# Token-major gates and branches, a finer hand-written order, and block transposes on VectorE in a two-layer hybrid decoder

## The chip, the cores and the metric

One core of one Trainium2 chip runs the whole program. The metric is device time in microseconds of one execution, as the median of the runs of a kernel. The core has five engines that work side by side, each on its own queue of instructions in order: TensorE (matmuls and transposes through the matmul array, into PSUM), VectorE, ScalarE (activation functions and copies), GpSimd (here only powers and a few fills), and SyncE (SP), which issues nearly all DMAs. The rows call them PE, DVE, ACT, POOL and SP; PEld is TensorE's weight load.

## The reference

The input is x, 256 tokens of 1024 features in float32. Each of two layers computes, with its own weights:

```
proj = x @ w_in                       # 1024 -> 7704 columns
ya = rg_lru(conv(proj[a])) * gelu(proj[a_gate])           # 512 wide
yb = rms_norm(gated_delta_rule(q, k, v)) * silu(proj[z])  # 512 wide
yc = rms_norm(gla(q, k, v)) * silu(proj[r])               # 512 wide
gates = sigmoid(proj[merge] + gate_b)                     # 3 x 1024
merged = sum(gates[b] * (y_b @ w_branch[b]) for b in (a, b, c))
x = layer_norm(alpha * x + merged @ w_out)
x = layer_norm(alpha * x + (silu(x @ w1) * (x @ w3)) @ w2)   # 2816 hidden
```

The gated delta rule solves, for each head and chunk of 64 tokens, a unit lower triangular system; the kernel builds the inverse from blocks of 8 up to 128.

## The kernel before

Every operand of a large product is split into a high and a low part of TensorE's fast float32 form, and each product is three matmuls: high x high, high x low, low x high. Weights come as 292 units of 128 x 1024 floats (512 KB), in the order of `ORDER`. `load_w` (line 402) issues a unit's DMA on SP into one of four `raw` buffers; `split_w` (line 415) makes the high part `hi` on ScalarE and the low part `lo` on VectorE, and then issues the next load; `unit` (line 441) hands out the next ready unit, after `fill` has brought the count of ready units up to `ahead` (6, and 14 from the first step of the last branch).

Two forms of product use a unit. Feature-major (`fm_acc`, `fm_pair`, line 1183) holds a 128x128 block of weights in the array and streams 256 tokens of x: 24 matmuls of 256 columns a unit, with features on the partitions of the result. Token-major (`tm_acc`, line 469, `tm_group`, line 1149) holds 128 tokens of x and streams 512 columns of weights: 12 matmuls of 512 columns a unit, with tokens on the partitions. The first FFN products of hidden columns from 512 up (`fm_acc2`, line 461, tile `f`) hold weights and stream the high and low part of x as one operand of 512 columns, and then the high part alone (256) against the low weights; in the tile of x (`xtile`, line 479) the high and low part of one block of 128 features lie 512 floats apart.

The order of work is written out by hand. `MIX` (line 42) lists the steps of a layer's mixer: `c`, `k`, `q`, `v`, `ax`, `ag`, `z` are projections, `gA0` to `gA3` the gates of branch A (each step 256 columns, two units), `bA0` the branch product of 256 columns (one unit), and so on for C and B. `main` (line 1191) walks the list and yields between units; everything else is a chain (a generator), such as `b_inv` (line 644, the inverse and what follows), `a_chain`, `c_chain`, `ln_chain` (line 1030). `Order` (from line 155) holds a model of each engine's clock. Its `drive` (line 211) traces, at each yield of `main`, the next step of a chain whose due time by the model has come. So the position of every instruction on its engine's queue is fixed when the program is traced. The SP queue is kept in the program's order.

Gates: `g_chain` (line 1003) applies a sigmoid with a per-feature bias on ScalarE, two activations of 128x256 a step. Branches: `m_chain` (line 1015) multiplies the product by the gate and adds it to `macc` on VectorE; after the last branch it splits the sum into `mh` and `ml`, which are the held operand of `wo`. `wo` runs the column halves one after the other; its last six units are done for the first 128 tokens and then for the second, so that the norm of the first runs beside the second.

Inverse: in `b_inv` `Y` is the transposed inverse so far, and `X` is its transpose. `X` is made three times a layer from blocks of at most 32, by 8 transposes on TensorE (tile `px`) and two copies on ScalarE.

## Time and profile before

| | us |
|---|---|
| median of 3 runs | 939.6 |
| lowest, highest | 938.99, 940.14 |
| the profiled execution | 940.46 |
| its span, first to last instruction | 938.7 |
| TensorE busy | 924.4 |
| VectorE busy | 642.0 |
| ScalarE busy | 527.6 |
| weight loads: 512 KB each, us to landing (median) | 4.4 |

The span runs from the first to the last instruction of the profiled execution; the rest of its time lies around it. Layer 0 runs to about 466 us. In it the projections run to about 120 us, the inverse stage beside the first gates to 174, branches and gates to 257, `wo` to 280, the FFN from there. The same stages of layer 1 begin at 466, end at 633, 721 and 744. Matmuls are pipelined, so the busy time of one is longer than the distance from one to the next; the chain in order of time shows that distance.

### The profile page before, as it was taken

Reading aid. Unit: us, or ns where it says so; the run is one execution under the profiler, and the core shown is the slowest. Engines: PE = TensorE matmul, PEld = TensorE weight load, DVE = VectorE, ACT = ScalarE, POOL = GpSimd, SP = SyncE. Lnnn points to the kernel's source line nnn. Section 1 sums busy time; section 2 is a strip of 40 time slices with the busy share of each in tenths; the row PEclk is TensorE's granted clock in tenths of the full one; section 3 lists DMA queues with packets and bytes.
Section 4 is the critical chain, followed back from the end, with each engine's and each line's share of the span. In section 5 each row is a group of like instructions: output and inputs, shape, how many; then the busy total and the mean of one; then the engine's idle time right before and its main releaser. Section 6 shows DMA issues by size and latency. Waiting matters only on the chain.

```text
span 938.7 us, 15760 instructions
## 1 busy us (share of the span) xinstructions
PE 924.4 (98%) x6306; PEld 840.3 (90%) x6306; DVE 642.0 (68%) x1017; ACT 527.6 (56%) x827; POOL 29.0 (3%) x29
## 2 busy tenths in 40 slices
PE   8999999999999999999999999999999999999996
PEld 5999999999988888888889999989999888888885
DVE  6778976675865776675557879574768658666715
ACT  5867679535724755565045864973457147555600
POOL 1000100000000000000000020000100000000001
PEclk9999999999999999999999999989999999999999
DMA  8855243545851865578144444234468248555801
GB/s 284 257 183 154 78 149 94 186 166 193 297 222 67 281 213 186 193 244 264 54 156 140 144 146 131 95 122 149 158 240 285 105 138 280 187 179 180 291 1 45
DMA packets 47993, 162.84 MB, mean 173 GB/s; under 512 B 7536, under 2 KB 8496, under 8 KB 47792
## 3 DMA queue, kind: packets, MB, share of 16 engines
q1 hardware_dynamic: 47776, 161.71, 51.5%
q8 instruction: 49, 0.80, 0.3%
q14 instruction: 24, 0.20, 0.1%
q10 hardware_dynamic: 144, 0.13, 0.0%
HBM read 160.77 MB, written 1.05 MB: 172 GB/s over the span
## 4 chain that ended last, share of the span: by engine, by line
PE 91%; ACT 4%; DVE 2%; DMA 1%; issue 1%; POOL 0%; SPq 0%; POOLq 0%; DVEq 0%; ACTq 0%
PE fm L346 25%; PE f L346 22%; PE w L346 13%; PE tm L346 11%; PE br L346 7%; PE wo L346 5%; DMA raw<-in_w_dram 1%; ACT L291 1%; PE pt L346 1%; PE pp L346 1%; DVE lo L303 1%; PE pln L354 1%; PE co L346 1%; ACT hi L291 1%; PE ptm L354 0%
## 5 line engine op out<-in xcount | busy, mean ns | idle before, releaser
L303 DVE TENSOR_TENSOR lo<-raw,hi 128x1024 fp32r<-128x1024 f32 (+1 forms) x293 | 350.8, 1217 | 94.4 <-ACT hi L291 88.1
L291 ACT ACTIVATE hi<-raw 128x1024 fp32r<-128x1024 f32 (+1 forms) x293 | 300.6, 1053 | 79.5 <-DMA raw<-in_w_dram 64.6
L346 PE MATMUL fm<-x,hi 128*128 128x256 f32 x1536 | 282.9, 286 | 0.0
L346 PEld LDWEIGHTS fm<-x,hi 128*128 128x128 f32 x1536 | 240.1, 192 | 2.3 <-issue 1.6
L346 PE MATMUL fm<-x,lo 128*128 128x256 f32 x768 | 217.6, 283 | 0.0
L346 PE MATMUL f<-x,hi 128*128 128x512 f32 x576 | 203.8, 399 | 0.0
L346 PE MATMUL f<-x,lo 128*128 128x256 f32 x576 | 161.8, 281 | 0.0
L346 PEld LDWEIGHTS fm<-x,lo 128*128 128x128 f32 x768 | 147.7, 192 | 0.0
L346 PEld LDWEIGHTS f<-x,hi 128*128 128x128 f32 x576 | 108.2, 188 | 26.9
L346 PE MATMUL w<-hi,hh 128*128 128x512 f32 (+1 forms) x396 | 111.1, 367 | 0.0
L346 PEld LDWEIGHTS f<-x,lo 128*128 128x128 f32 x576 | 108.8, 189 | 0.1
L346 PE MATMUL tm<-hi,x 128*128 128x512 f32 x320 | 100.7, 398 | 2.1 <-ACT hi L291 2.1
L346 PEld LDWEIGHTS w<-hi,hh 128*128 128x128 f32 x396 | 71.4, 189 | 12.3
L346 PEld LDWEIGHTS tm<-hi,x 128*128 128x128 f32 x320 | 59.3, 190 | 15.3 <-ACT hi L291 3.8
L346 PE MATMUL w<-lo,hh 128*128 128x512 f32 (+1 forms) x198 | 72.4, 366 | 0.0
L346 PE MATMUL tm<-lo,x 128*128 128x512 f32 x160 | 62.2, 392 | 0.1
L291 ACT ACTIVATE gt<-fm,vecs 128x256 f32<-128x256 f32 x48 | 20.5, 470 | 48.0 <-PE fm L346 48.0
L346 PEld LDWEIGHTS w<-lo,hh 128*128 128x128 f32 x198 | 37.3, 188 | 6.2
L291 ACT ACTIVATE x<-pln 128x256 fp32r<-128x256 f32 x24 | 7.9, 383 | 61.7 <-PE pln L354 61.7
L346 PE MATMUL wo<-hi,mh 128*128 128x512 f32 x128 | 39.8, 392 | 0.0
L303 DVE TENSOR_TENSOR hv<-f,hv 128x256 f32<-128x256 f32 x36 | 15.2, 422 | 31.4 <-ACT hv L291 31.4
L346 PEld LDWEIGHTS tm<-lo,x 128*128 128x128 f32 x160 | 30.2, 189 | 7.1 <-DVE lo L303 0.7
(276 smaller groups left out, 1081.8 us busy)
## 6 DMA issues: line engine op xcount, KB each, us to landing
raw<-in_w_dram SPq DMA_DIRECT2D x291, 512.0 KB, 4.4
lnv<-in_lnv_dram SPq DMA_DIRECT2D x8, 512.0 KB, 8.0
xr<-in_xtm_dram SPq DMA_DIRECT2D x1, 1024.0 KB, 7.4
xin<-in_xfm_dram SPq DMA_DIRECT2D x3, 256.0 KB, 7.0
raw<-in_w_dram SPq DMA_DIRECT2D x2, 256.0 KB, 3.4
ar<-in_aw_dram SPq DMA_DIRECT2D x8, 64.0 KB, 3.9
out_dram<-xr SPq DMA_DIRECT2D x2, 256.0 KB, 2.1
kc<-in_kc_dram SPq DMA_DIRECT2D x1, 476.0 KB, 8.9
```

What stands on the lines that cost most here:

```text
L291: ins_ = A.activation(o, i, f, **k)
L303: V.tensor_tensor(out=o, in0=a, in1=b, op=op)
L346: T.matmul(o, w, x, start=start, stop=stop)
L354: T.transpose(o, i, idn)
```

## The change

The gates become token-major: a step is now 512 columns (four units), the bias is added on VectorE from a tile `gbias` that is broadcast over the partitions by a DMA of 512 KB (one for each branch and layer), and a sigmoid of 128x512 follows on ScalarE. The branch products become token-major too, two units a step. The merged sum is therefore token-major; it is transposed on TensorE (tile `pmt`) and split from PSUM into `mh` and `ml`. `wo` runs by rows of its weights first and columns second, and waits for the merged halves `mrg00`, `mrg01`, `mrg10`, `mrg11`. The prefetch depth grows by 1 at the two C steps, by 2 at the two B steps, and to 14 at `wo`.

The order's model now keeps, for each piece of a tile, who wrote and read it and when, and takes due times from that; its costs are new; token-major groups, feature-major units and `w2` yield after half a unit. In the tiles of x the high and low part of a block of 128 features lie side by side. The three transposes of the inverse become one `transpose` of 128x1024 in blocks of 32x32 on VectorE (`flip`).

Not shown below: the packing of weights and bias in the new order, the cost terms of the remaining helpers (each now names its operands), and the same in the loads at the start.

```diff
-MIX = ("c0 c1 ax0 k0 k1 q0 z0 q1 ax1 v0 v1 ag0 ag1 gA0 gA1 gA2 gA3 bA0 bA1 bA2 bA3 "
-       "gC0 bC0 gC1 bC1 gC2 bC2 gC3 bC3 gB0 gB1 bB0 bB1 gB2 bB2 gB3 bB3").split()
+MIX = ("c0 c1 ax0 k0 k1 q0 z0 q1 ax1 v0 v1 ag0 ag1 gA0 gA1 bA0 bA1 gC0 bC0 gC1 bC1 "
+       "gB0 gB1 bB0 bB1").split()
...
-            o += fm(C_MG + 1024 * b, i) if nm[0] == "g" else [("br", b, i)]
-    o += [("wo", n, q) for n in range(2) for q in range(4)]
+            o += tm(C_MG + 1024 * b + 512 * i) if nm[0] == "g" else [
+                ("br", b, i, q) for q in range(2)]
+    o += [("wo", n, q) for q in range(4) for n in range(2)]
...
-    def op(self, eng, cost, ready=0.0):
-        t = max([self.clk[eng], self.ready, ready] +
-                [f for e, f in self.fin.items() if e != eng])
-        t += cost
-        self.clk[eng] = t
-        self.fin[eng] = t
+        self.ready = self.last = ready
+
...
+    def op(self, eng, occ, tail=0.0, out=None, ins=(), ready=0.0):
+
+        t = max(self.clk[eng], self.ready, ready)
+        for a in ins:
+            t = max(t, self.after(eng, a, False))
+        if out is not None:
+            t = max(t, self.after(eng, out, True))
+        self.clk[eng] = t + occ
+        f = t + occ + tail
...
+        return f
+
     def end(self):
-        return max(list(self.fin.values()) + [self.ready])
+        return self.last
...
-    def dve(o, x=0.0):
-        O.op("dve", 0.13 + x + 0.00104 * n_of(o))
+    def dve(o, *i, x=0.0):
+        n = max(n_of(a) for a in (o,) + i)
+        ps = any(a.space == bass.MemoryType.PSUM for a in i)
+        O.op("dve", 0.045 + x + 0.057 * ps + 0.00104 * n, 0.105, o, i)
...
+    def flip(o, i):
+
+        V.transpose(o, i)
+        dve(o, i)
...
         if w.dtype == F32R:
-            O.op("pe", max(n, m, 128) / 2400.0)
+            c = max(n, 2 * m) / 2400.0 + 0.0135
         else:
-            O.op("pe", max(n, m, 32) / 600.0)
+            c = max(n, m, 24) / 600.0 + 0.01
+        O.op("pe", c, 0.16, o, (w, x))
 
     def tp(o, i, idn):
         T.transpose(o, i, idn)
-        O.op("pe", 0.107)
+        O.op("pe", 0.109, 0.16, o, (i,))
...
-    def load_w(between=None):
+    def dma(o, i, free=0.0):
+        nc.sync.dma_start(out=o, in_=i)
+        O.clk["dma"] = max(O.clk["dma"], free + 1.5)
+        keep, O.ready, last = O.ready, 0.0, O.last
+        f = O.op("dma", o.shape[0] * n_of(o) * 4 / 285e3, 0.5, o)
+        O.ready, O.last = keep, last
+        return f
...
+        t = raws.pop(0)
...
     def xtile(name):
-        v = [slot(name, F32R).rearrange("p (q k c) -> p k q c", q=2, k=2) for _ in range(4)]
+        v = [slot(name, F32R).rearrange("p (k q c) -> p k q c", q=2, k=2) for _ in range(4)]
         return [t[:, :, 0] for t in v], [t[:, :, 1] for t in v], v
...
             tt(YT.rearrange("p (t b i) -> p t b i", t=8, b=16),
                z[:, :, None, :].to_broadcast([P, 8, 16, 8]), b16, MULT)
             yield
-            for tk in range(2):
-                px = h4(bank("px"))
-                for h in range(4):
-                    tp(px[:, h], Y[tk][:, h], ident)
-                cp(X[tk], px)
+            flip(XT, YT)
...
                 yield
-                for tk in range(2):
-                    px = h4(bank("px"))
-                    for h in range(4):
-                        tp(px[:, h], Y[tk][:, h], ident)
-                    cp(X[tk], px)
+                flip(XT, YT)
...
-        def g_chain(ps, b, j):
-            ps = p2(ps)
-            if j % 2 == 0:
-                B["gt", b, 0], B["gt", b, 1] = pair2("gt")
-            gt = B["gt", b, j % 2]
-            for t in range(2):
-                act_fn(gt[:, t], ps[:, t], AF.Sigmoid, bias=vc(V_GB + 8 * b + 2 * j + t))
-            B["gg", b, j] = gt
-            done(f"gt{b}{j}")
-            return
-            yield
-
-        def m_chain(ps, n, b, j, mh, ml):
-            yield k_(f"gt{b}{j}")
-            ps = p2(ps)
-            gt = B["gg", b, j]
+        def g_tm(ps, b, j, tk, bias):
+            if tk == 0:
+                B["gt", b, j] = pair("gt")
+            gt = B["gt", b, j][tk]
+            tt(gt, ps, bias[:, 512 * j:512 * j + 512], ADD)
+            yield
+            act_fn(gt, gt, AF.Sigmoid)
+            done(f"gt{b}{j}{tk}")
+
+        def m_tm(ps, n, b, j, tk, mh, ml):
+
+
+            yield k_(f"gt{b}{j}{tk}")
+            gt = B["gt", b, j][tk]
             if n == 0:
-                if j % 2 == 0:
-                    B["macc", j], B["macc", j + 1] = pair2("macc")
-                tt(B["macc", j], ps, gt, MULT)
-            else:
-                tt(gt, ps, gt, MULT)
-                tt(B["macc", j], B["macc", j], gt, ADD)
-            if n == 2:
-                split(mh[j], ml[j], B["macc", j])
-                done(f"mrg{j}")
+                if j == 0:
+                    B["macc", tk] = pair("macc")
+                tt(B["macc", tk][j], ps, gt, MULT)
+                return
+            tt(gt, ps, gt, MULT)
+            acc = B["macc", tk][j]
+            tt(acc, acc, gt, ADD)
+            if n == 1:
+                return
+            yield
+            pt = h4(bank("pmt"))
+            for q in range(4):
+                tp(pt[:, q], acc[:, q * P:(q + 1) * P], ident)
+            for q in range(2):
+                split(*(x[2 * j + q][:, :, tk * P:(tk + 1) * P] for x in (mh, ml)),
+                      pt[:, 2 * q:2 * q + 2])
+            done(f"mrg{j}{tk}")
...
                         w = unit(2)
                         for tk in range(2):
                             tm_acc(ps[tk], x, tk, w, 2 * q, q == 0, q == 3)
-                        if q == 3:
-                            for tk in range(2):
+                            if q == 3:
                                 O.spawn(chain(ps[tk], tk), 1)
-                        yield
+                            yield
...
                             fill()
-                        if q % 2:
-                            yield
+                        yield
...
-                fm_acc(p2(ps)[:, t], unit(8), xs)
-                if t:
-                    O.spawn(chain(ps), prio)
-                yield
+                w = unit(8)
+                for k in range(0, 8, 4):
+                    fm_acc(p2(ps)[:, t], w, xs, k, k + 4)
+                    if t and k:
+                        O.spawn(chain(ps), prio)
+                    yield
...
                     b = "ABC".index(nm[1])
-                    yield from fm_pair(lambda ps: g_chain(ps, b, i), 1)
+                    if i == 0:
+                        bias = slot("gbias")
+                        nc.sync.dma_start(out=bias, in_=ins["gb"][
+                            l:l + 1, 1024 * b:1024 * b + 1024].to_broadcast([P, 1024]))
+                    yield from tm_group(xs, [
+                        lambda ps, tk: g_tm(ps, b, i, tk, bias)], None)
                 else:
                     n, b = BRANCHES.index(nm[1]), "ABC".index(nm[1])
+                    if n == 1:
+                        ahead[0] = min(ahead[0] + 1, FAR)
                     if n == 2:
-                        ahead[0] = FAR
+                        ahead[0] = min(ahead[0] + 2, FAR)
                     y = ("ya", "yb", "yc")[b]
                     yield k_(y)
                     y = B[y]
-                    w = unit(4)
-                    ps = bank("br")
-                    for t in range(2):
-                        fm_acc(p2(ps)[:, t], w, y, slice(P * t, P * t + P))
-                    O.spawn(m_chain(ps, n, b, i, mh, ml), 1)
-                    yield
+                    ps = [bank("br") for _ in range(2)]
+                    for q in range(2):
+                        w = unit(2)
+                        for tk in range(2):
+                            tm_acc(ps[tk], y, tk, w, 2 * q, q == 0, q == 1)
+                            if q:
+                                O.spawn(m_tm(ps[tk], n, b, i, tk, mh, ml), 1)
+                            yield
...
-            seq = [(n, q) for n in range(2) for q in range(4)]
+            ahead[0] = FAR
+            seq = [(n, q) for q in range(4) for n in range(2)]
...
             tail = 6
             for i in range(8 - tail):
-                yield k_(f"mrg{i}")
+                yield k_("mrg00"), k_("mrg01")
                 w = unit(2)
                 for tk in range(2):
                     wo(i, w, tk)
+                    yield
             u = []
             for tk in range(2):
                 for i in range(8 - tail, 8):
+                    if seq[i][1] == 2:
+                        yield k_(f"mrg1{tk}")
                     if tk == 0:
-                        if i < 4:
-                            yield k_(f"mrg{i}")
...
                 for tk in range(2):
                     for n in range(len(pw[tk])):
                         w2(j, w, tk, n)
-                yield
+                    yield
```

## Rows read from the trace of the kernel before

**Rows 1.** Page: busy time of engines (us, share, instructions), the last chain's shares.

```profile
PE 924.4 (98%) x6306; PEld 840.3 (90%) x6306; DVE 642.0 (68%) x1017; ACT 527.6 (56%) x827; POOL 29.0 (3%) x29
...
PE 91%; ACT 4%; DVE 2%; DMA 1%; issue 1%; POOL 0%; SPq 0%; POOLq 0%; DVEq 0%; ACTq 0%
```

**Rows 2.** Chain that ended last, in order of time: start us, us, what, matmuls.

```profile
178.93 8.63 PE br L346 x72
...
222.98 11.52 PE fm L346 x96
...
309.72 96.10 PE f L346 x544
405.82 55.82 PE w L346 x246
...
478.60 10.91 PE tm L346 x48
```

**Rows 3.** The same chain: inverse stage of layer 0, then the stall of layer 1.

```profile
134.76 1.79 PE pt L346 x16
...
140.86 0.89 PE px L354 x8
...
615.36 3.95 PE fm L346 x24
```

**Rows 4.** Timeline of PE: start us, us, instruction, count, idle before and releaser.

```profile
610.64 1.90 PE L346 MATMUL pt<-pb,X 128*128 128x128 f32 x8 [1.79 <-ACT pb L291]
613.28 2.08 PE L346 MATMUL pt<-pb,X 128*128 128x128 f32 x8 [0.74 <-ACT pb L291]
```

**Rows 5.** Windows: length, busy us (instructions) of each engine, PEclk, DMA share, GB/s.

```profile
120.00:150.00 30.00, 29.57 (x315) 28.92 (x315) 18.40 (x30) 25.92 (x45) 0.00 (x0) 1.00 0.33 98
585.00:615.00 30.00, 27.47 (x223) 26.98 (x222) 16.65 (x22) 29.79 (x49) 0.00 (x0) 0.93 0.33 113
610.64:613.28 2.64, 1.90 (x8) 1.61 (x8) 1.42 (x2) 2.63 (x5) 0.00 (x0) 0.54 0.30 64
613.28:617.70 4.42, 4.42 (x20) 4.42 (x21) 2.77 (x5) 4.39 (x7) 0.00 (x0) 0.50 0.42 140
```

**Rows 6.** Timeline of PE: transposes between `wo` matmuls; a turn from 256 to 512.

```profile
277.44 0.66 PE L354 MATMUL pln<-kc,xr 128*128 128x128 f32 x4
...
278.17 0.39 PE L346 MATMUL wo<-lo,mh 128*128 128x512 f32 x1
...
905.69 0.63 PE L346 MATMUL w<-hi,hh 128*128 128x512 f32 x2
...
907.76 0.40 PE L346 MATMUL w<-hi,hh 128*128 128x256 f32 x2
```

**Rows 7.** Groups by line and shape: count, busy us, mean ns, idle before.

```profile
L291 ACT ACTIVATE gt<-fm,vecs 128x256 f32<-128x256 f32 x48 | 20.5, 470 | 48.0 <-PE fm L346 48.0
L291 ACT ACTIVATE X<-px 128x512 f32<-128x512 f32 x12 | 6.5, 605 | 1.5 <-PE px L354 1.5
...
L303 DVE TENSOR_TENSOR gt<-br,gt 128x512 f32<-128x512 f32 x16 | 11.0, 685 | 3.9 <-PE br L346 3.9
L303 DVE TENSOR_TENSOR Y<-sub,kc 128x1024 f32<-128x1024 f32 x2 | 2.5, 1226 | 0.1
```

**Rows 8.** Windows, as rows 5: branches and gates after branch A, layers 0 and 1.

```profile
180.00:257.50 77.50, 77.50 (x649) 77.50 (x648) 55.75 (x69) 42.08 (x55) 1.64 (x1) 1.00 0.63 217
657.00:721.20 64.20, 64.20 (x537) 64.19 (x536) 49.31 (x61) 36.47 (x47) 2.54 (x1) 1.00 0.66 222
```

**Rows 9.** Tile `lnv`, the 8 broadcast loads of 512 KB.

```profile
DMA to landing us min/median/max: 7.2/8.0/9.0
```

**Rows 10.** Layer 1's last `yal` (ns min/median/max, starts), then the chain's branch A.

```profile
L303 DVE TENSOR_TENSOR yal<-gl,yah x2: 686/689/692, 629.2 to 629.8; 128x512 fp32r<-128x512 f32 x2
...
633.25 3.07 PE br L346 x24
```

**Rows 11.** Timeline of DVE: the first norm's first operation.

```profile
271.21 0.69 DVE L314 SCALAR_TENSOR_TENSOR xr<-xr,wo 128x512 f32<-128x512 f32 x1 [5.28 <-PE wo L346]
```

More of the change, by code (lines that the diff above doesn't have):

```diff
@@ L168, in begin, with span, after @@
     def begin(self, ready):
-        self.ready = ready
-        self.fin = {}
-    def op(self, eng, cost, ready=0.0):
-        t = max([self.clk[eng], self.ready, ready] +
-                [f for e, f in self.fin.items() if e != eng])
-        t += cost
-        self.clk[eng] = t
-        self.fin[eng] = t
-        return t
+        self.ready = self.last = ready
+    @staticmethod
+    def span(ap):
+        pitch = ap.ap[0][0]
+        p0, c0 = divmod(ap.offset, pitch) if pitch else (0, 0)
+        p1 = p0 + ap.ap[0][1]
+        dims = [d for d in ap.ap[1:] if d[1] > 1]
+        runs = [c0]
+        if len(dims) > 1 and dims[0][1] <= 4:
+            runs = [c0 + dims[0][0] * k for k in range(dims[0][1])]
+            dims = dims[1:]
+        n = sum(st * (k - 1) for st, k in dims) + 1
+        return ap.tensor.name, [(p0, p1, c, c + n) for c in runs]
+    def after(self, eng, ap, write):
+        name, rects = self.span(ap)
+        t = 0.0
+        for q0, q1, d0, d1, f, e, w in self.mem.get(name, ()):
+            if (w or write) and not e == "pe" == eng and any(
+                    q0 < p1 and p0 < q1 and d0 < c1 and c0 < d1 for p0, p1, c0, c1 in rects):
+                t = max(t, f if e == eng else f + 0.03)
+        return t
+    def op(self, eng, occ, tail=0.0, out=None, ins=(), ready=0.0):
[6 more added lines that the diff above has]
+        f = t + occ + tail
+        self.last = max(self.last, f)
+        for a in ins:
+            name, rects = self.span(a)
+            self.mem.setdefault(name, []).extend((*r, f, eng, False) for r in rects)
+        if out is not None:
+            name, rects = self.span(out)
+            m = self.mem.setdefault(name, [])
+            m[:] = [x for x in m if not any(
+                p0 <= x[0] and x[1] <= p1 and c0 <= x[2] and x[3] <= c1
+                for p0, p1, c0, c1 in rects)] + [(*r, f, eng, True) for r in rects]
+        return f
     def end(self):
-        return max(list(self.fin.values()) + [self.ready])
+        return self.last
     def spawn(self, gen, prio, ready=None):
@@ L400, in halves, with load_w @@
         return [slice(c, c + n) for c in range(0, 1024, n)]
-    def load_w(between=None):
+    def dma(o, i, free=0.0):
[5 more added lines that the diff above has]
+        return f
+    def load_w(between=None, free=0.0):
         i = len(raws) + pos[1]
@@ L408, in load_w @@
         for c in halves(i):
-            nc.sync.dma_start(out=t[:, c], in_=ins["w"][l, j][:, c])
+            dma(t[:, c], ins["w"][l, j][:, c], free)
             if i == 0 and c.start == 0:
                 between()
-        O.clk["dma"] = max(O.clk["dma"], O.clk["pe"] - 4.0) + 1.5
-        raws.append((t, O.clk["dma"] + 2.0))
+        raws.append(t)
     def split_w(between=None):
@@ L417, in split_w @@
             return
-        t, at = raws.pop(0)
+        t = raws.pop(0)
         i = pos[1]
         pos[1] += 1
-        keep = O.ready, O.fin
-        O.begin(at)
+        keep = O.ready, O.last
+        O.begin(0.0)
         hi, lo = slot("hi", F32R), slot("lo", F32R)
@@ L430, in split_w @@
         tt(lo_, t_, hi_.bitcast(F32), SUB)
-        ready.append((hi, lo, O.end()))
-        O.ready, O.fin = keep
-        load_w()
+        ready.append((hi, lo))
+        at = O.end()
+        O.ready, O.last = keep
+        load_w(free=at)
     held, ahead = [0], [AHEAD]
```

64 lines of the change are left out of this document (34 added, 30 removed).

## The prediction

> **What bounds the kernel now.** I read the page's engine rows first: TensorE is busy for 924.4 of 938.7 us, and the chain of work that ended last runs through TensorE for 91% [rows 1]. So most of the span is a queue of matmuls, and an edit is worth what it takes out of that queue or out of the few holes in it. The chain in order of time then gives each kind of matmul its spacing, which is a better price than the busy time of one, since matmuls overlap: 96 feature-major gate matmuls (256 columns) in 11.52 us are 0.1200 us each, 72 branch matmuls in 8.63 us are 0.1199, and 48 token-major ones (512 columns) in 10.91 us are 0.2273 [rows 2]. Twice 0.1200 is more than 0.2273: for the same number of columns the long form is 5% cheaper.
>
> The holes are the ends and one stall. TensorE idles after 930.7 us while the last norm runs, and the first stretch waits for data; the change alters no work in either. The stall is in layer 1, in the inverse stage: TensorE idles 1.79 us and then 0.74 us for ScalarE's copies `pb` [rows 4], and its granted clock then reads 0.54 and 0.50, that is the 1.2 GHz level instead of 2.4 [rows 5]. From 608.85 us, where it runs dry, to 619.31, where the unit behind the stall ends [rows 3], pass 10.46 us; the work in it is 16 matmuls `pt` (1.79 us where undisturbed) and one gate unit (24 x 0.1200 = 2.88) [rows 2, 3]. The stall therefore costs 10.46 - 4.67 = 5.8 us. Layer 0 loses only the 0.43 us of its window [rows 5]. Together 6.2 us. Around the stall ScalarE is busy for 29.79 of 30 us, against 25.92 of 30 in layer 0 [rows 5].
>
> **The change part by part.**
>
> *Gates and branches token-major.* A weight unit is now 24 matmuls x 0.1200 = 2.88 us, and becomes 12 x 0.2273 = 2.73, so 0.152 us less. Units that change: 24 gate and 12 branch units a layer, 72 in all: 72 x 0.152 = 10.9 us, all on the path, since TensorE has no idle time in those stages. Bounds: at the spacing that the 512-column matmuls have in `f`, where a 256-column one stands between (0.3533 - 0.1200 = 0.2333, below), a unit is 2.80 and the sum 5.8 us; at 55.82 / 246 = 0.2269 [rows 2] it is 11.3. I take 10.9: the token-major row has the same shapes in the same sequence.
>
> The Trainium skill speaks against this price (TensorE: Matmul & The Clock Gate, Back-to-back issue gap): at full clock the gap is the columns over 2.4 GHz plus 2.5 ns, about 109 ns at 256 columns and 216 ns at 512. By it the 72 units would give only about 2.2 us. The rows show 11 ns more than it at either size, so the trace disagrees with it.
>
> *Transposes that this adds.* The merged sum is now token-major, so each of its 8 half tiles (2 column halves x 2 token halves x 2 layers) takes 4 transposes before `wo`. Four transposes between `wo` matmuls, with the slower matmul after them, take 278.17 - 277.44 = 0.73 us, of which 0.23 is that matmul: 0.50 x 8 = 4.0 us added [rows 6].
>
> *Inverse's transposes to VectorE.* 6 groups of 8 transposes leave TensorE: 0.89 us each [rows 3], 5.3 us removed. With the line before, the net of transposes is -1.3 us. ScalarE loses 12 copies `X` of 0.605 us (3.6 a layer) [rows 7]. VectorE gains 6 block transposes of 128x1024; the trace has none, so from below 0.69 us each (the 128x512 product `gt`) and from above twice the 1.23 of the 128x1024 product `Y` [rows 7]; I take 1.23, the row of its size: 7.4 us beside TensorE's work. They also take a trip through TensorE's queue out of the inverse's chain.
>
> *Gate bias and sigmoid.* 48 sigmoids with bias (20.5 us) become 24 of 512 columns, each about 0.6 us like the 512-column copies `X` [rows 7]: about 6 us less there. VectorE gains 24 additions of 0.69 us (the `gt` row), 16.4 us. In the stage after the A branch VectorE is busy 55.75 of 77.5 us in layer 0 and 49.31 of 64.2 in layer 1 [rows 8]; 8 of the additions fall there per layer (5.5 us), while TensorE's share shrinks by 4.0 and 3.3 us (26 and 22 of the 72 units lie there) and grows by 4 x 0.50, so about 61 of 75 and 55 of 63. That is cover for them, thinner than before; where it is gone, an addition costs its 0.69. What queues behind an addition on VectorE is the `lo` halves of coming weights, and TensorE waits for those only when the six units ahead are used up.
>
> The six bias loads (512 KB each) go onto SP's queue between weight loads. The loads of the same form (`lnv`) land in 7.2 to 9.0 us [rows 9]; the first reader comes after four units, 10.9 us. Nothing there, so long as SP gets its slot at once.
>
> *Adjacent x parts.* In `f` 544 matmuls take 96.10 us [rows 2]: 0.3533 for a pair of 512 and 256 columns, against 0.2273 + 0.1200 = 0.3473, an excess of 6.0 ns; 576 pairs make 3.5 us. Either the 512-column operand in two runs costs it, and adjacency removes it, or the turn from 256 back to 512 columns does. The second is seen without any split operand: in the last layer's `w`, nine contiguous 512-column matmuls that follow 256-column ones take 907.76 - 905.69 = 2.07 us, not 9 x 0.2273 = 2.05 [rows 6], 20 ns for a turn. So I take 0, and 3.5 as the other end.
>
> The skill has a rule for the other end (Advanced Engine Details and Errata, PSUM Cachelines): any access pattern with holes slows matmuls markedly. No run here shows it for an operand of two long runs.
>
> *Order and prefetch.* Half-unit steps, a due time from real dependencies, `ahead` in steps of 1 and 2 instead of one leap to 14: none changes an instruction of TensorE. What they can do is move the 6.2 us. All of it may go, or another stall like it may come (+5.8). ScalarE is what the stall waits for, and its load before the A branch falls by 3.6 us of copies and about 1.4 of sigmoids (8 of 0.47 become 4 of 0.6); but what is late next stands close behind: `yal` is ready at 630.5 us, and the A branch starts at 633.25 [rows 10]. Without the stall and with 8 gate units shorter by 0.152, TensorE comes there 7.0 us sooner, 4.2 us before that `yal`, while ScalarE's relief is 5.0. With both layers' orders drawn anew I take half of the 6.2: -3.1.
>
> *wo by rows first.* Both column halves of a token half now end with the last two units, so the norm's first half can't start early. It doesn't now either: its first operation starts at 271.21, when the token half's sum is complete [rows 11]. Zero; 1.4 us a layer (two operations of 0.69) if it did use it. What is new is that `wo` waits for transposes: the first merged half has the four half units of the last branch step (5.5 us) to hide in, the second six half units of `wo` (8.2 us), and its own chain is about 3.5 us (two VectorE operations of 0.69, 0.50 of transposes, two pairs of 128x256 copies); zero, and up to 2 us a layer if three `lo` halves stand ahead of it.
>
> Sum: -10.9 - 1.3 - 3.1 = -15.3 us. The profiled execution took 940.46 us (938.7 and 1.76 around it), so 925.2; the median is 0.86 below that execution: **924.3 us**.
>
> **The rivals.**
> - *Stall gone and `f` gains:* order frees ScalarE wholly (-6.2), or adjacency is real (-3.5). 939.6 - 12.2 - 6.2 - 3.5 = 917.7 with both, about 921 with one. For it: ScalarE's relief; against it: the turn in `w`.
> - *Stall stays or moves to the A branch:* 939.6 - 12.2 = 927.4; with another of the kind 933.2. For it: `yal` is late next.
> - *Spacing follows columns:* the units save less because something besides the count of matmuls paces them; with the 5.8 us of the bound, 929.4, and with the 2.2 of the page about 933. The rows speak against it.
> - *Slower:* in the inverse stage the finer steps put more of the chains' work before the weight splits in ScalarE's and VectorE's queues, and TensorE runs dry again and again. Place: 120 to 150 us and 585 to 615 us, where ScalarE has 4 and 0 us free in 30. Price: 5.8 us a time, idle and half clock together. Two such stalls beyond today's leave 927.4 + 11.6 = 939.0, no change; from three on it is slower, 944.8. Against it: ScalarE's load there falls.
>
> **How the numbers follow.** Forecast 924.3 (about 922 to 927): 0.45. Stall gone or `f` gaining (917.5 to 922): 0.24. Stall stays or moves (927 to 933): 0.18; spacing follows columns (929 to 933): 0.05. No change: 0.04. Slower: 0.04. Range 917 to 932: it takes in the bounds of `f` and of the stall, and leaves out the top of the stall and spacing cases and the last two. 0.2% of the time, 1.9 us, is about what a measurement of this kernel can tell from no change. Faster 0.92, same 0.04, slower 0.04.
>
> **What the profile after would show.** Gates and branches: token-major rows at 0.227 us spacing, no 256-column rows for gates. Transposes: no `px`, 8 groups `pmt`. `f`: 0.353 or 0.347 a pair. Stall: every granted clock of layer 1 at 2.4 GHz, no idle TensorE before the A branch. I am wrong if TensorE is idle for more than some 10 us inside the layers, or if its 512-column matmuls in the gates are spaced over 0.23.

## The result, and the profile after

The changed kernel takes 920.6 us (median of four runs, 918.5 to 921.9) where the kernel before takes 939.9: a ratio of 0.978, 95% interval 0.9761 to 0.9799. That is 19.3 us less; the forecast was 924.3, or 15.3 less than the 939.6 it was reckoned from. The profiled execution took 919.68 us with a span of 917.9, so the spans differ by 20.8 us (938.7 before). The steps below are held against that 20.8.

The page of the kernel after: the row of the engines (busy us, share, instructions) and the shares of the chain that ended last.

```profile
PE 905.8 (99%) x5426; PEld 789.0 (86%) x5426; DVE 663.3 (72%) x1055; ACT 512.0 (56%) x795; POOL 28.2 (3%) x29
...
PE 98%; DMA 1%; DVE 0%; issue 0%; SPq 0%; ACT 0%; POOL 0%; POOLq 0%
```

Beside [rows 1], TensorE is busy 18.6 us less, and the chain now runs through it for 98%, not 91: the holes of the mixer are gone too. The chain in order of time says where the rest went (start us, us, what, matmuls).

```profile
12.39 10.00 PE tm L394 x36
...
217.58 21.76 PE tm L394 x96
239.34 10.88 PE br L394 x48
250.22 1.31 PE pmt L403 x12
...
298.22 5.65 PE f L394 x32
...
304.31 94.30 PE f L394 x544
398.60 55.80 PE w L394 x246
...
754.44 94.30 PE f L394 x544
```

Gates and branches are now token-major at 21.76 / 96 = 0.2267 us, against two times 0.1200 before [rows 2]. The feed-forward's first stage `f` runs its long stretch of 544 matmuls in 94.30 us, which is 0.3467 a pair and not 0.3533. Its first 32 matmuls, ahead of a group of four transposes (`pht`), still take 5.65 us, or 0.353 a pair, as before. `w` is as it was. The first line is a loss: those 36 matmuls of the start took 8.45 us in the profile of the kernel before.

The windows of the kernel after (length, then busy us and instructions of PE, PEld, DVE, ACT and POOL, then PEclk, DMA share, GB/s): two stretches of the inverse stage, that answer to [rows 5], one of the start, and the stretch from the first gate behind branch A to `wo`, in both layers, that answers to [rows 8].

```profile
120.00:150.00 30.00, 30.00 (x219) 28.30 (x219) 23.49 (x35) 27.36 (x42) 2.54 (x1) 1.00 0.32 109
570.00:600.00 30.00, 30.00 (x218) 28.21 (x217) 22.84 (x35) 27.96 (x43) 1.64 (x1) 1.00 0.34 121
12.40:16.00 3.60, 3.60 (x9) 2.88 (x10) 2.39 (x4) 2.63 (x3) 0.00 (x0) 0.54 0.76 242
180.44:251.53 71.09, 71.09 (x342) 59.64 (x340) 57.00 (x73) 37.33 (x44) 1.64 (x1) 1.00 0.72 249
632.40:701.67 69.27, 69.27 (x325) 57.82 (x323) 56.16 (x71) 37.62 (x44) 1.64 (x1) 1.00 0.73 248
```

TensorE is never idle in the inverse stage and its granted clock stays at the 2.4 GHz level, although ScalarE is still busy for 27 to 28 of 30 us: the stall of [rows 4] is gone without ScalarE having become free. VectorE is at 57.0 of 71.1 and 56.2 of 69.3 us in the stages behind branch A, the thinner cover that was expected. In the start, from 12.4 to 16 us, the granted clock reads 0.54.

The groups by line and shape (count, busy us, mean ns, idle before), that answer to [rows 7]:

```profile
L346 DVE TENSOR_TENSOR gt<-tm,gbias 128x512 f32<-128x512 f32 x24 | 16.2, 685 | 5.1 <-PE tm L394 5.0
L331 ACT ACTIVATE gt<-gt 128x512 f32<-128x512 f32 x24 | 14.8, 628 | 20.6 <-DVE gt L346 20.6
L378 DVE STREAM_TRANSPOSE X<-Y 128x1024 f32<-128x1024 f32 x6 | 7.4, 1238 | 0.1
```

The three prices taken from neighbours were 0.69, 0.6 and 1.23 us; they are 0.685, 0.628 and 1.238.

From the chain's start times, stage by stage (us, before and after):

| stretch | before | after | difference |
|---|---|---|---|
| start to the first feature-major matmul, layer 0 | 32.48 | 34.22 | +1.74 |
| from there to the long stretch of `f`, layer 0 | 277.24 | 270.09 | -7.15 |
| long `f` stretch, layer 0 | 96.10 | 94.30 | -1.80 |
| layer 1's first unit to its long `f` stretch | 306.85 | 294.90 | -11.95 |
| long `f` stretch, layer 1 | 96.10 | 94.30 | -1.80 |

They sum to -20.96; the rest (`w`, the norms, the end) makes +0.16.

### The profile page after: what moved, and what is told of

The parts are those of the page before. It is cut to its first block, busy times and chain, and to the rows that moved or that the text cites. A ratio compares the mean times of both kernels' runs of the same rounds, so it can differ in the third digit from the quotient of the medians.

```text
span 917.9 us, 14007 instructions
## 1 busy us (share of the span) xinstructions
PE 905.8 (99%) x5426; PEld 789.0 (86%) x5426; DVE 663.3 (72%) x1055; ACT 512.0 (56%) x795; POOL 28.2 (3%) x29
## 4 chain that ended last, share of the span: by engine, by line
PE 98%; DMA 1%; DVE 0%; issue 0%; SPq 0%; ACT 0%; POOL 0%; POOLq 0%
PE tm L394 26%; PE f L394 22%; PE fm L394 15%; PE w L394 13%; PE br L394 7%; PE wo L394 5%; PE pt L394 1%; PE pp L394 1%; DMA raw<-in_w_dram 1%; PE pln L403 1%; PE pr L394 1%; PE ptm L403 1%; PE co L394 1%; PE pss L394 0%; PE pat L394 0%; PE pa L394 0%
## 5 line engine op out<-in xcount | busy, mean ns | idle before, releaser
L394 PE MATMUL tm<-hi,x 128*128 128x512 f32 x704 | 221.0, 396 | 2.7 <-ACT hi L331 2.7
L394 PE MATMUL f<-x,hi 128*128 128x512 f32 x576 | 200.2, 392 | 0.0
L394 PEld LDWEIGHTS tm<-hi,x 128*128 128x128 f32 x704 | 130.7, 189 | 30.7 <-ACT hi L331 4.5
L394 PE MATMUL fm<-x,hi 128*128 128x256 f32 x768 | 141.3, 286 | 0.0
L394 PE MATMUL tm<-lo,x 128*128 128x512 f32 x352 | 137.6, 393 | 0.0
L394 PEld LDWEIGHTS fm<-x,hi 128*128 128x128 f32 x768 | 119.7, 192 | 1.8 <-issue 1.6
L394 PE MATMUL fm<-x,lo 128*128 128x256 f32 x384 | 108.6, 283 | 0.0
L394 PEld LDWEIGHTS tm<-lo,x 128*128 128x128 f32 x352 | 66.6, 189 | 14.7 <-DVE lo L346 0.7
L394 PEld LDWEIGHTS fm<-x,lo 128*128 128x128 f32 x384 | 73.6, 192 | 0.0
L357 DVE SCALAR_TENSOR_TENSOR xr<-xr,w 128x512 f32<-128x512 f32 (+1 forms) x9 | 5.6, 627 | 39.0 <-PE w L394 39.0
```

Source lines behind the costliest of these rows:

```text
L357: V.scalar_tensor_tensor(out=o, in0=a, scalar=s, in1=b, op0=op0, op1=op1)
L394: T.matmul(o, w, x, start=start, stop=stop)
```

## The experiments

Each time is the median beside runs of the kernel before on the same chip. Where a profile is compared, spans are: 938.7 before, 917.9 after. Parts were first done alone on the kernel before (b_), then undone alone in the kernel after (a_). One execution of each kernel was profiled. The kernel after was not run again beside the a_ runs, so a difference to its 920.6 can be up to 2 us off the difference of the spans.

### Adjacent x parts alone: b_adj

```
-        v = [slot(name, F32R).rearrange("p (q k c) -> p k q c", q=2, k=2) for _ in range(4)]
+        v = [slot(name, F32R).rearrange("p (k q c) -> p k q c", q=2, k=2) for _ in range(4)]
```

> The kernel before with one edit: the high and the low half of each x tile stand side by side, so that the 512-wide moving operand of a pair in the feed-forward's first stage is one run of 512 instead of two runs of 256. Theory A, two runs cost time (it rests on the kernel after, where a pair of that stage fell from 0.3533 to 0.3467 us): 544 pairs x 0.0066 = -3.6 us, time 936.3, the stage's two chain groups 94.3 us each. Theory B, the turn from a 256-wide to a 512-wide matmul costs it (the step of the prediction): no change, 939.9 us, the groups stay at 96.1.

941.7 us beside 941.0, ratio 1.0009 (0.9997 to 1.0021). The chain's rows of `f`:

```profile
310.02 96.10 PE f L346 x544
...
773.45 96.10 PE f L346 x544
```

Not a hundredth changes: theory A falls. The layout alone does not give the 3.6 us that `f` gave in the kernel after.

### The turn from 256 to 512 columns: b_turn

```
-        for k in range(nk):
-            mm(o, w[0][:, k], x[2][k // 2][:, k % 2], k == 0, False)
-            mm(o[:, 0], w[1][:, k], xk(x[0], k), False, k == nk - 1)
+        for k in range(0, nk, 2):
+            for j in (k, k + 1):
+                mm(o, w[0][:, j], x[2][j // 2][:, j % 2], j == 0, False)
+            for j in (k, k + 1):
+                mm(o[:, 0], w[1][:, j], xk(x[0], j), False, j == nk - 1)
```

> The kernel before with the order of the feed-forward's first stage changed: two 512-wide matmuls, then two 256-wide ones, so that there are half as many turns from 256 to 512; the operands and their layout stay as they were. Theory B, the turn costs it: half of 1088 turns x 0.0066 or so goes, -3.6 / 2 = -1.8 us, and the two chain groups of the stage fall from 96.1 to about 95.2 us each. Theory A, two runs in the operand cost it: no change, 96.1 each, 939.9 us.

937.8 us, ratio 0.997 (0.9959 to 0.9981).

```profile
311.20 94.75 PE f L346 x544
...
774.07 94.76 PE f L346 x544
```

Same operands in two runs, half the turns, 1.35 us less in each layer; the 32 matmuls ahead of the stretch fall too, from 5.65 to 5.57 us. So the order of the two widths costs time, as the prediction said, but it gives more than the expected half (0.9). (The two stretches have 544 turns back to 512 columns and not 1088; the expected 1.8 us in both is half of 544 x 0.0066.)

### The block transposes alone: b_flip

```
-            for tk in range(2):
-                px = h4(bank("px"))
-                for h in range(4):
-                    tp(px[:, h], Y[tk][:, h], ident)
-                cp(X[tk], px)
+            flip(XT, YT)
```

(At both places; `flip` is the block transpose of the kernel after.)

> The kernel before with one edit: the three transposes per layer of the inverse's matrix go to VectorE as one block transpose of 128x1024 each; order model, gates and branches stay as they were. Both theories take the 6 groups of transposes off TensorE: 6 x 0.89 = -5.3 us. Theory R (ScalarE's relief cures the stall: the 3.6 us of copies per layer that ScalarE had in that stage are gone): the stall of the second layer goes too, -5.3 - 6.2 = -11.5 us, time 928.4, granted clock 1.00 through the second layer. Theory O (the order cures it): a stall stays in the inverse stage of the second layer, -5.3 us alone, 934.6, and the clock falls there as in the kernel before.

943.8 us, ratio 1.0025 (1.0011 to 1.0039): a little slower, and neither theory. Windows of this run, columns as above, and the wait of TensorE behind the last of them, that ends after 630 us (who waits for whom, us, times, longest):

```profile
120.00:135.00 15.00, 13.28 (x115) 13.09 (x114) 13.46 (x20) 12.79 (x15) 0.00 (x0) 1.00 0.60 203
...
165.00:180.00 15.00, 13.63 (x119) 13.04 (x118) 11.38 (x19) 7.41 (x12) 0.99 (x2) 1.00 0.44 144
...
585.00:600.00 15.00, 13.10 (x104) 12.63 (x104) 11.21 (x17) 13.82 (x17) 0.00 (x0) 0.93 0.63 220
...
615.00:630.00 15.00, 12.82 (x171) 12.51 (x170) 13.03 (x18) 11.96 (x21) 0.00 (x0) 0.96 0.58 172
```
```profile
PE pp L351 <- DVE Y L318: 2.2, 1, 2.2
```

TensorE runs dry in four places, twice in the layer that had no stall worth the name. From layer 1's first unit to its long `f` stretch it takes 308.8 us instead of 306.85, where 2.7 us of transposes had left. With ScalarE relieved and the order's model as before, there are more stalls, not fewer, and in the two windows of layer 0 TensorE still waits for ScalarE (1.7 us for `pb`, then 0.7 each for `kd` and `w`): ScalarE's relief alone does not cure. Whether it is the new place of the chain's steps or the longer step on VectorE that opens each hole was not separated.

### The new order alone: b_order

The kernel after with the other parts undone. What is left beside the kernel before is the model of engine times and dependencies, the half-unit yields, prefetch in steps, and `wo` by rows:

```
+                for k in range(0, 8, 4):
+                    fm_acc(p2(ps)[:, t], w, xs, k, k + 4)
...
+                    if n == 1 and i % 2 == 0:
+                        ahead[0] = min(ahead[0] + 1, FAR)
```

> The kernel before with the new order alone: the new model of engine times and dependencies, yields by half units, the stepwise prefetch and the new order of the output projection; gates and branches feature-major, transposes on TensorE, x layout as before. Theory O (the order cures the stall of the second layer): -6.2 us, 933.7, no idle time of TensorE and granted clock 1.00 in the inverse stage of the second layer. Theory R (only ScalarE's relief cures it): the stall stays, 0 to -1 us, 939 to 940. In both the startup may cost up to 1.6 us more, if the granted clock falls there as in the kernel after.

932.0 us, ratio 0.991 (0.989 to 0.9929): -8.9, more than theory O. The chain's `f`, then the windows of the inverse stage of layer 1:

```profile
310.38 94.30 PE f L393 x544
...
766.43 94.30 PE f L393 x544
```
```profile
585.00:600.00 15.00, 15.00 (x158) 14.69 (x158) 8.18 (x11) 13.02 (x23) 0.00 (x0) 1.00 0.35 106
600.00:615.00 15.00, 15.00 (x178) 14.56 (x177) 14.16 (x23) 13.01 (x19) 0.00 (x0) 1.00 0.39 131
```

No idle time and full clock, with the transposes and ScalarE's copies still there: the order, taken as a whole, cures the stall. From layer 1's first unit to `f` it is 300.85 us against 306.85, so -6.0. Another 3.6 is `f`, with x still in two runs; 0.5 is lost at the start.

### Gates and branches feature-major again: a_fm

```
-                    yield from tm_group(xs, [
-                        lambda ps, tk: g_tm(ps, b, i, tk, bias)], None)
+                    yield from fm_pair(lambda ps: g_chain(ps, b, i), 1)
```

(With the units, the bias column and the merge of the kernel before.)

> The kernel after with gates and branches feature-major again (48 gate units of 24 and 24 branch units of 24 matmuls of 256 columns, the gate bias on ScalarE), all else as in the kernel after. Theory T (the price of the prediction holds): the spacing costs 72 units x 0.152 = +10.9 us and the 8 groups of the merged tile's transposes save 4.0: +6.9 us, time 927.5, idle time of TensorE as in the kernel after. Theory C (the token-major form costs or saves cover elsewhere too: 24 additions of 0.685 us less on VectorE, per-token halves that start earlier): the difference from 927.5 is more than 1.5 us, and an idle time of TensorE above that of the kernel after, or below it, shows it.

926.6 us, ratio 0.9837 (0.9823 to 0.9852): +6.0 by the medians. The span is 925.4, +7.5, of which 0.58 lies before the first feature-major matmul: +6.9, the price of theory T. By the chain's start times 3.6 and 3.5 of it lie ahead of the long stretch of `f` in layers 0 and 1. TensorE is not idle between 525 and 660 us here either. The chain:

```profile
221.64 11.52 PE fm L393 x96
233.16 5.76 PE br L393 x48
```

### Transposes back on TensorE: a_noflip

The edit of b_flip the other way round, in the kernel after.

> The kernel after with the inverse's transposes on TensorE again (6 groups of eight transposes, ScalarE copies). Theory T: 6 x 0.89 = +5.3 us and no stall, because the new order covers it: 925.9. Theory R (ScalarE's relief, not the order, keeps the stall away): +5.3 and a stall in the inverse stage of the second layer of 6 us, 932, the granted clock below 1.00 there. Theory F (the block transposes' 1.24 us is a longer step in the chain than the transposes were, and is exposed in part): less than +3 us.

925.4 us, ratio 0.9824 (0.9809 to 0.9839), +4.8 by the medians; the span is 923.1, +5.2, against 5.3 in theory T. The windows show no stall:

```profile
135.00:150.00 15.00, 15.00 (x172) 13.49 (x171) 8.98 (x13) 12.87 (x21) 0.00 (x0) 1.00 0.42 143
...
585.00:600.00 15.00, 15.00 (x183) 14.21 (x183) 8.64 (x16) 13.02 (x21) 0.00 (x0) 1.00 0.25 76
```

Having the transposes on VectorE is worth 5.2 us with the new order and less than nothing with the old.

### Yields by whole units: a_whole

```
                 for k in range(0, 8, 4):
                     fm_acc(p2(ps)[:, t], w, xs, k, k + 4)
-                    if t and k:
-                        O.spawn(chain(ps), prio)
-                    yield
+                if t:
+                    O.spawn(chain(ps), prio)
+                yield
```

(And so in the token-major units, the branches, `wo` and `w`.)

> The kernel after with yields by whole units again (feature-major units of 24 matmuls, token-major units of both token tiles, down projections of both), the model of times and dependencies as in the kernel after. Theory M (the model alone cures the stall): no idle time of TensorE beyond that of the kernel after, 920.6 +- 1 us. Theory H (the half units are what cures it, since a step of the inverse's chain can wait up to 2.9 us for the end of a unit): TensorE idles some 2 to 6 us in the inverse stages, 923 to 927 us. In both the feed-forward's pair stays at 0.3467 us if the output order of that stage is unchanged.

930.3 us, ratio 0.9878 (0.9861 to 0.9894): +9.7, beyond theory H; the span is 928.1, +10.2. Windows, and TensorE's longest wait in 165 to 180 us (a wait stands where it ends):

```profile
150.00:165.00 15.00, 13.09 (x142) 11.21 (x140) 12.31 (x17) 13.24 (x19) 0.00 (x0) 1.00 0.48 165
165.00:180.00 15.00, 12.83 (x65) 11.02 (x66) 8.68 (x19) 5.27 (x9) 0.99 (x2) 0.54 0.07 26
...
615.00:630.00 15.00, 13.58 (x136) 10.91 (x135) 10.72 (x20) 10.33 (x16) 0.00 (x0) 1.00 0.52 163
```
```profile
PE pp L394 <- DVE Y L361: 2.5, 2, 2.3
```

In layer 0 TensorE is idle 1.9 and 2.2 us in these windows, most of it for the inverse's `Y` on VectorE, and the granted clock reads 0.54 in the second. In layer 1 it is idle 1.4 us, for ScalarE's `w` and `kd`, at full clock. By the chain's start times 9.6 us lie in layer 0, between its first feature-major matmul and the long stretch of `f`, and 1.7 in layer 1. So without the finer steps the chain falls out of step in layer 0, where the kernel before lost only 0.4 us; in layer 1, where that had its stall, the model goes most of the way without them. `f` is at 94.30 in both layers.

### One more transpose: b_tp5

```
             for q in range(4):
                 tp(ps[:, q], t[:, q * P:(q + 1) * P], ident)
+            tp(ps[:, 3], t[:, 3 * P:4 * P], ident)
```

> The kernel before with one more 128x128 transpose behind each of the four groups of transposes of the first feed-forward tile (a repeat of the last one, so that the result is the same); nothing else. In the kernels before, with the x parts side by side, and with block transposes a pair of the feed-forward's first stage takes 0.3533 us; with the new order, and after, 0.3467; TensorE's instructions there differ by one, a wait between the last group of these transposes and the first matmul behind it. Theory P (which of two rhythms the pairs run in follows from the number of instructions in front of them): 0.3467, the two long chain groups 94.3, -3.6 + 4 x 0.11 = -3.2 us, 936.7. Theory W (it is the wait itself, or something else of the order): 0.3533 and 96.1 still, +0.4 us, 940.3.

942.4 us, ratio 1.0005 (0.9995 to 1.0015).

```profile
311.53 96.10 PE f L346 x544
```

Theory P falls.

### A PSUM bank skipped: b_skip and a_skip

```
+                    if f == 5 and chain is f_gate:
+                        for _ in range(1):
+                            tp(bank("skip")[:, 0:P], ident, ident)
                     ps = p2(bank("f13"))
                     fm_acc2(ps, unit(8), x1)
```

> The kernel before with one PSUM bank skipped ahead of the third unit of the feed-forward's first stage: one 128x128 transpose of the identity goes into the skipped bank, and the unit gets a bank for which TensorE has to wait on an earlier operation of its own, so that a wait stands as an instruction of its own between the transposes and the unit's first matmul. In the kernel before there is none there; in the kernel after and in the run with the new order alone there is one. Theory W (that wait sets which rhythm the pairs run in): 0.3467 us a pair, the two long chain groups at 94.3, -3.6 + 0.2 = -3.4 us, 936.5. Theory S (something else of the new order sets it): 0.3533, 96.1 still, +0.2 us, 940.1.

941.8 us, ratio 1.0007 (0.9991 to 1.0023). With the wait put in, layer 0 stays and layer 1 gains:

```profile
310.03 96.11 PE f L346 x544
...
774.00 94.30 PE f L346 x544
```

> The kernel after with the same skip of a bank: here it takes the unit to a bank that needs no wait of TensorE on itself, so that the wait as an instruction of its own ahead of the unit's first matmul is gone (the transpose into the skipped bank carries it). Theory W: the pairs go back to 0.3533 us, the two long chain groups to 96.1, +3.6 + 0.2 = +3.8 us, 924.4, although the two parts of x lie side by side. Theory S: 0.3467 and 94.3 still, 920.8.

923.5 us, ratio 0.9811 (0.9797 to 0.9826), span 921.2. With the wait taken away, both layers lose:

```profile
303.89 96.10 PE f L394 x544
...
755.97 96.10 PE f L394 x544
```

a_skip goes as theory W said; b_skip does so in one layer only, and the two runs below have the wait in both layers and 96.10 in layer 0. So the wait alone doesn't decide it either. That x lies in one run is no help in a_skip: a second time the layout drops out.

### The prefetch in one leap: a_leap

```
-                    if n == 1:
-                        ahead[0] = min(ahead[0] + 1, FAR)
                     if n == 2:
-                        ahead[0] = min(ahead[0] + 2, FAR)
+                        ahead[0] = FAR
```

> The kernel after with the old prefetch step: the number of weight units held ahead goes to 14 at once at the first step of branch B, in place of one or two more at a step. Theory N (the prediction: the steps cost and bring nothing, ScalarE and VectorE have room there): 920.6 +- 0.5 us, TensorE never idle in the branch stage. Theory L (a burst of eight splits, 1.05 us each on ScalarE and 1.22 on VectorE, stands in front of the gates' additions and sigmoids): TensorE waits for gates in the branch stage, +1 to +6 us.

936.1 us, ratio 0.9945 (0.9924 to 0.9966): +15.5, far above both; the span is 935.2, +17.3. TensorE does not wait for a gate there, it waits for the last merge. TensorE in the windows at the end of the branch stage of both layers, its waits from 236 to 262 us, and the timeline of DVE there (start us, us, instruction, count):

```profile
240.00:255.00 15.00, 10.24 (x49) 8.21 (x48) 13.29 (x17) 8.16 (x10) 0.00 (x0) 0.97 0.85 287
...
705.00:720.00 15.00, 9.62 (x39) 7.75 (x38) 13.43 (x22) 8.31 (x16) 0.00 (x0) 0.71 0.81 269
```
```profile
PE pmt L403 <- DVE macc L346: 4.8, 2, 3.6
```
```profile
247.06 1.22 DVE L346 TENSOR_TENSOR lo<-raw,hi 128x1024 fp32r<-128x1024 f32 x1
248.20 1.28 DVE L346 TENSOR_TENSOR gt<-tm,gbias 128x512 f32<-128x512 f32 x2
249.40 1.21 DVE L346 TENSOR_TENSOR lo<-raw,hi 128x1024 fp32r<-128x1024 f32 x1
250.53 0.68 DVE L346 TENSOR_TENSOR gt<-br,gt 128x512 f32<-128x512 f32 x1
251.13 1.21 DVE L346 TENSOR_TENSOR lo<-raw,hi 128x1024 fp32r<-128x1024 f32 x1
252.26 0.68 DVE L346 TENSOR_TENSOR macc<-macc,gt 128x512 f32<-128x512 f32 x1
```

TensorE has finished its last branch at about 249 us. The additions of the last gate start only at 248.20, though its products were done at 238: `lo` halves of later weights stand ahead of them on VectorE's queue, and one stands ahead of nearly each step that follows. Three of the four pieces of the sum are still to be made, and `wo` needs their transposes. The stage behind `wo`'s start then runs partly at the lower clock (0.81 from 255 to 270 us). By the chain's start times the mixer is 6.5 and 7.6 us longer than in the kernel after, the stage from `wo` to the next 1.3 in either layer, and layer 0's `f` is at 96.10 here (1.8).

### A warm start: a_warm

```
+                            if l == 0 and q == 0 and tk and chain is chains[0] and len(chains) > 1:
+                                pw = bank("warm")
+                                for _ in range(7):
+                                    T.matmul(pw, warm[:, 0:P], warm, start=True, stop=True)
```

> The kernel after with seven more matmuls of 512 columns on a zeroed bf16 tile behind the first unit, where TensorE waits 1.75 us for the second unit's weights and in the profile of the kernel after the granted clock then is 0.54 from 12.4 to 16.0 us. Theory G (the idle time is what lets the clock fall): granted clock 1.00 in 12.4 to 20 us, the first token-major stretch 8.5 us long in place of 10.0, -1.5 us against the profile of the kernel after, and -0.5 to -1.5 in the median, since the clock does not fall in each execution. Theory D (it delays the second unit as much as it saves): 0 +- 0.5 us.

920.5 us, ratio 0.978 (0.9766 to 0.9795), span 918.2: no gain over the kernel after. The window of the start, then `f`:

```profile
12.40:16.00 3.60, 3.60 (x17) 2.94 (x16) 3.21 (x5) 1.87 (x4) 0.00 (x0) 1.00 1.01 295
```
```profile
302.78 96.10 PE f L394 x544
...
754.76 94.30 PE f L394 x544
```

The clock reads 1.00, and the first feature-major matmul starts at 32.66 us instead of 34.22, -1.56, as theory G said. One profile cannot show that the added matmuls did it: the clock reads 1.00 there in 6 of the 13 other profiles too (see the end). Layer 0's `f` is back at 96.10, +1.8. The two cancel in this execution, so no version beats the kernel after.

## Why the prediction was right or wrong, point by point

**What bounds the kernel: right.** TensorE's queue was the bound and is so still. The parts, measured one at a time by the spans, give a sum that closes: order 9.0 (b_order's span), token-major 6.9 (a_fm), transposes 5.2 (a_noflip), layout 0 (b_adj): 21.1, against 20.8. It closes to 1 or 2 us only, since the start alone moves by that much from one profile to the next.

**Token-major: right.** The price of the 512-column row came out as 0.2267 instead of 0.2273 us. With the transposes that it adds, 10.9 - 4.0 = 6.9 was forecast and a_fm shows 6.9 by the chain, 6.0 by the medians. The formula that was weighed against it, which the Trainium skill gives for a matmul by itself (TensorE: Matmul & The Clock Gate, Back-to-back issue gap), would have given 2.2 of the 10.9. The rows disagree with it, at 226.7 ns for 512 columns.

**Transposes to VectorE: right in size, wrong in what it rests on.** 5.3 was forecast and 5.2 found, but only under the new order; alone the edit costs 2 to 3 us (ratio 1.0025). The prediction's rival "slower", TensorE running dry again and again in the inverse stage, is what happened to this part when it came without the order (b_flip). The prediction listed the parts as if each had a price of its own.

**The stall: the mechanism was wrong, and the size half.** Half of 6.2 us was taken, since it was open whether it would move. All of it went. The prediction leaned on ScalarE's relief; b_flip shows that relief without a cure, and b_order a cure without it. Which part of the order cures layer 1 is not separated: without the half-unit steps (a_whole) layer 1 loses 1.7 us only. What those steps do hold off is a stall in layer 0, which at 9.6 us costs more than the one of the kernel before. The prediction took them for something that shifts the stall about, and did not see that the kernel after could not do without them.

**`f`: the step on the layout was right, the sum still lacked 3.6 us.** The step took 0 for adjacency and named the turn from 256 to 512 columns instead. b_adj shows 0, and b_turn shows that fewer turns are cheaper. So the Trainium skill's rule that spoke for a gain (Advanced Engine Details and Errata, PSUM Cachelines: access with holes slows matmuls) does not show for an operand of two runs of 256. The section is about PSUM, and this operand lies in SBUF. What the step missed is that this cost of the turn is not fixed: the same pairs of matmuls run at 0.3533 or 0.3467 us through a whole stretch, and the kernel after has the second. What decides between the two stays open. 0.3467 is the sum of the two spacings without any turn (0.2267 + 0.1200).

**Prefetch in steps: the zero held, but hid a condition.** Beside the kernel before, where TensorE does not idle in the branch stage with the leap, there was nothing for the steps to gain. In the kernel after, the leap in their place costs 15.5 us (a_leap): the other parts' gain rests on them. The working had the mechanism, `lo` halves ahead of the last merge on VectorE, and a price of up to 2 us a layer for three of them. It did not ask what the old leap would do to the new additions; the measured price is 6.5 and 7.6 us a layer, and more behind it at the lower clock.

**`wo` by rows, bias loads, VectorE's additions: zeros that hold.** The bias loads land in 4.3 to 5.8 us, and TensorE has no wait for a gate or for the merge. From `wo`'s first matmul to the next stage it takes 23.4 us in both layers, where it was 22.8 and 23.1. The difference, 0.9 us in all, is one group of `pmt` transposes a layer (0.43 and 0.44 us) that now lies between `wo`'s matmuls; the 4.0 us of the forecast has them already.

**Not foreseen: the start.** The first 36 token-major matmuls took 10.00 instead of 8.45 us at a lower granted clock. Variants of both kernels show it in some profiles and not in others, so it is not put down to the change: see below.

Put together: the forecast was 3.1 short on the stall and 3.6 short on `f`; in the profiled execution 1.7 at the start went the other way. Together that makes 20.3 of the 20.8 us. The median, 920.6, lies below the band of the forecast (922 to 927) and in that of the rival "stall gone and `f` gains" (917.5 to 922, chance 0.24). Both of the rival's gains came, but not for its reasons: the order takes the stall away without ScalarE's relief too (b_order), and adjacency gives `f` nothing (b_adj). That the forecast came within 4 us is in part luck: two of its terms were too small, and a loss that it did not have made up for some of that.

## What to carry to other kernels

Price a change's parts in the kernel that will hold them all: the transposes alone made the kernel before slower, and the leap of the prefetch, which cost it no idle time, cost 15.5 us in the kernel after. When an edit puts work on an engine that also prepares coming weights, ask what stands ahead of that work on its queue, and how deep the prefetch may run at that point. And where the stream of matmuls is the bound, let the chains interrupt it in short steps: here half units (1.4 us) in place of whole ones (2.7 to 2.9) decided 9.7 us, nearly all of it in one layer.

## What the runs showed of the hardware that was not expected

**A stretch of alternating 512- and 256-column matmuls keeps one of two spacings.** In 13 kernels of this form (all but b_turn), the 26 long stretches of `f` took 96.10 or 94.30 us each, to 0.01, nothing between: 96.10 in both layers of the kernel before, b_adj, b_flip, b_tp5 and a_skip; 94.30 in both layers of the kernel after, b_order, a_fm, a_noflip and a_whole; 96.10 in layer 0 and 94.30 in layer 1 of b_skip, a_leap and a_warm. The 32 matmuls of `f` ahead of the four transposes in front of each stretch take 5.64 or 5.65 us in all 26 cases, 0.353 a pair, so the faster spacing begins only behind those transposes. Nor is the excess of the slower one the same at each turn: read from the trace to the nanosecond, the pairs of the kernel before last about 350, 350 and 361 ns in turn through the whole stretch, those of the kernel after 346 or 347 each. The layout of the operand (b_adj), the number of matmuls ahead (b_tp5) and a wait in front of the stretch (b_skip, a_skip) were tried as the cause and none decides it. Each kernel was profiled once, so whether a kernel's spacing changes from one execution to the next is not shown either. The cause stays open, and 1.8 us a layer hang on it: an effect of that size between two versions of this kernel proves nothing until `f` is read.

**The clock at the start falls in half of the profiles.** TensorE waits 1.3 to 2.7 us for the second unit's weights in each of the 13 profiles that have no work put into that gap. In 7 of them the granted clock then reads between 0.54 and 0.73 from 12.4 to 16 us, after waits of 1.75 to 2.69 us, and in the other 6 it reads 1.00, after waits up to 2.54 us. So the length of the wait doesn't decide it alone. The Trainium skill (TensorE: Matmul & The Clock Gate, The HAM clock gate) says that how many matmuls run at the lower level at a kernel's start varies from run to run. Here it is a fall behind a gap soon after the start that comes or does not, in profiles of kernels whose start is nearly the same; a like variation, at another place. With seven matmuls on zeros in the gap the clock reads 1.00 in the one profile that has them, which alone doesn't show that they keep it up.
